# Two MLP layers whose tokens' operands leave out 1/rms, with Winograd products in the first block too

## The chip, the cores and the metric

One core of a Trainium2 chip runs the whole program in one launch. The metric is the device time of one execution in microseconds; the median of several executions counts.

## The reference

A trunk of two layers over 1024 tokens with 1024 features, all in float32: HGRN2 (a gated linear recurrence) and an MLP, then a shared compressed K/V, multi-head latent attention (MLA), a second MLP, and a last norm. What the change is about is the MLP, which occurs twice:

```python
def rmsnorm(x, gain):
    return x * lax.rsqrt(jnp.mean(x * x, axis=-1, keepdims=True) + EPS) * gain

def sq_relu_mlp(xn, w_up, w_down):                 # 1024 -> 4096 -> 1024
    return jnp.square(jax.nn.relu(xn @ w_up)) @ w_down

h = h + hgrn2_mixer(rmsnorm(h, ...), ...)
h = h + sq_relu_mlp(rmsnorm(h, mlp_norm[0]), mlp_w_up[0], mlp_w_down[0])
...
h = h + mla_mixer(rmsnorm(h, ...), ..., k_nope, k_rope, v, cos, sin)
h = h + sq_relu_mlp(rmsnorm(h, mlp_norm[1]), mlp_w_up[1], mlp_w_down[1])
return rmsnorm(h, final_norm)
```

1/rms is one positive number a token. It can therefore be taken out of the relu: relu(x r) = r relu(x), and out of the square as r squared.

## The kernel before

The tokens lie in two halves u = 0, 1 of 512; the stream `hT[u]` (tile `res` in the profile) holds the features on the partitions, in 8 tiles of 128x512. The stages follow one another: HGRN2 to about 672 us, the first MLP to 1345, K/V and attention to 2167, the second MLP and the last norm to the end. Within a stage a scheduler puts the instructions of each engine into one order ahead of time, by the order in which the code states them, by `tc.issue_after`, and by the rooms of the pools; at run time every engine works its queue in order.

**Products.** Every float32 operand is used as a high part (a cast to the matmul's type) and a low part (what the cast leaves out, by a subtraction); a product is three terms, high by high, high by low, low by high. `product` (L620) multiplies 512 features by 128 columns of weights and 512 tokens so: 12 matmuls of 128x512. `times` (L751) does a product of `down`: 24 matmuls into four banks of PSUM, then four additions to the stream on VectorE (L758). `parts` (L610 the cast on ScalarE, L534 the subtraction on GpSimd or VectorE) makes a weight's two parts, `halves` (L583, L534) the tokens'. In the profile `wh`, `wl` are weights' parts, `wu` and `dn` the raw rooms of w_up and w_down, `hh`, `hl` the parts of `down`'s inner operands, `fr` the room of the inner features, and `xn`, `T2h`, ..., `T4l` the tokens' parts; `ps`, `mm` and `nb` are PSUM banks.

**An MLP** takes the 4096 inner features in 8 blocks of 512. In each, `up` makes the inner features in two halves of 256, by Winograd's scheme in 7 products of half-size blocks (of tokens' features B11, B21, B22 and sums T1 to T4, of weights A11 to A22 and sums), then relu and square; `down` takes w_down's quarters and the inner features' quarters through 7 products x1 to x7, in the order x1, x5, x3, x6, x7, x4, x2, whose results add up in two sets of banks p and q. The very first up is `up_plain`: 16 products without Winograd's sums, the first token half before the second. Ahead of it `inverse(u)` takes the squares of the half's features (L560), adds them, multiplies with ones (L565), takes the logarithm and exponential and one Newton step, and `normed` (L577) multiplies the stream by gain and 1/rms. In layer 1 `finish.turn` transposes the stream in place, so that `down` adds with the tokens on the partitions: 64 transposes (L1170) and 16 copies out of PSUM (L1174 VectorE, L1176 ScalarE); they lie in `up_plain`.

```python
def down(A, s, last):                               # before, L763
    x1 = operands(A11, B11)
    ...
    q = times(s, x1, True, [(0, 0)])
    p = times(1 - s, x5, True, [(1, 1)])
    times(p, x3, False, [(1, 0)])
    times(q, x6, False, [(1, 0)])
    times(q, x7, False, [(1, 1)])
    times(q, x4, False, [(0, 1)])
    times(1 - s, x2, True, [(0, 0)])
```

Of the kernel before, what the change touches and what calls it, by code (L numbers as in the profile page):

```python
# [8 lines left out]
F32 = mybir.dt.float32  # L9
# [46 lines left out]
def build(nc, tc, a):  # L56
# [26 lines left out]
    ones = const.tile([P, P], F32R, name="ones")  # L83
    onef = const.tile([P, P], F32, name="onef")
    V.memset(onef, 1.0)
    V.tensor_copy(out=ones, in_=onef)
    eps = const.tile([P, 1], F32, name="eps")
    V.memset(eps, EPS)
    masks = const.tile([P, 640], U8, name="masks")
    m_diag = masks[:, 0:128]  # L90
    m_h1 = masks[:, 128:192]
    m_h2 = (masks[:, 192:256], masks[:, 256:320])
    m_lv = {h: masks[:, 320 + 64 * i:384 + 64 * i] for i, h in enumerate(LEVELS)}
    tri = const.tile([P, P], U8, name="tri")
    negt = const.tile([P, P], F32, name="negt")
    V.memset(negt, NEG)
# [80 lines left out]
    with common("hg"), tc.tile_pool(name="hg", bufs=1, reuse_waits="tile") as hp, \  # L177
            tc.tile_pool(name="hgp", bufs=1, space=PSUM, reuse_waits="tile") as pp:
        gn = vecs[:, R_GN:R_GN + 1]
        o_all = [None, None]  # L180

# [60 lines left out]
        lb, oml = const.tile([P, 8], F32, name="lb"), const.tile([P, 8], F32, name="oml")  # L242
# [208 lines left out]
        DMA.dma_start(out=mf[:, :640 + P], in_=a["masks"])  # L451
        G.tensor_copy(out=masks, in_=mf[:, :640])
        G.tensor_copy(out=tri, in_=mf[:, 640:640 + P])
# [53 lines left out]
    def mlp(layer, gain, finish):  # L507
# [5 lines left out]
        with ExitStack() as pools:  # L513
            mt, md, mf, mu, mw, mh, mp = (pools.enter_context(tc.tile_pool(name=f"mlp{n}{layer}", bufs=1,
                                                                           reuse_waits="tile")) for n in "tdfuwhp")
# [29 lines left out]
            X["T2"], X["B12"] = extra("T2"), extra("T4")  # L545
# [3 lines left out]
            for u, t in enumerate((fr, dn)):  # L549
# [4 lines left out]
            inv = s_y[:, 0], s_z[:, 0]  # L554

            def inverse(u, mark=None):
                acc, s, y, t = s_a[:, 0], s_a[:, 1], inv[u], s_y[:, 1]
# [6 lines left out]
                if mark is None:  # L564
                    T.matmul(ps, onef, acc, start=True, stop=True)  # L565
                else:
                    with tc.high_priority(offset=1000), tc.issue_after(mark):
                        T.matmul(ps, onef, acc, start=True, stop=True)
# [12 lines left out]
            def halves(eng, key, src):  # L581
                for k in (slice(0, 2), slice(2, 4)):
                    S.copy(out=X[key][0][:, k], in_=src[:, k])  # L583
                    sub(eng, X[key][1][:, k], src[:, k], X[key][0][:, k].bitcast(F32))

            def combine(eng, out, x, y):
                for k in (slice(0, 2), slice(2, 4)):
                    sub(eng, out[:, k], x[:, k], y[:, k])
# [12 lines left out]
            inverse(0, marks[-5 if finish is None else -14])  # L601
            normed(0, 0)
            halves(V, "B11", f[0, 0])
            normed(1, 0)
            halves(V, "B21", f[1, 0])

            def parts(eng, x, room=None):
                wh, wl = room or (small("wh"), small("wl"))
# [19 lines left out]
            def relu(o, src=None):  # L628
                S.activation(out=o, in_=o if src is None else src, func=AF.Relu)
                square(o)  # L630

            def up_plain(A, C):


                tiles = [(1, 0), (1, 1), (0, 0), (0, 1)]
                acc = {}
                room = extra("T3")
                w = {}
                for n, (e, i) in enumerate(tiles):
                    w[n, 0] = parts(G, A[e][i, 0], tuple(r[:, n, :] for r in room))  # L640
                    w[n, 1] = parts(G, A[e][i, 1])

                def step(n, u, k):
                    return product(acc[n, u], w[n, k], ("B11", "B21", "B12", "B22")[2 * u + k], k == 0, k == 1)

                def out(n, u):
                    e, i = tiles[n]
                    relu(C[e][i, u], acc[n, u])

                done = {}  # L650
                for n in range(4):
                    acc[n, 0], = banks_of(0, 1)
                    for k in range(2):
                        done[n] = step(n, 0, k)
                if finish is not None:
                    finish.turn(0, banks_of, done[1])
                inverse(1)
                normed(0, 1)
                halves(V, "B12", f[0, 1])
                normed(1, 1)  # L660
                halves(V, "B22", f[1, 1])
                if finish is not None:
                    finish.turn(1, banks_of, done[3])
                order = (2, 3, 0, 1)
                for n, b in zip(order, banks_of(1)):
# [594 lines left out]
```

## Time and profile before

| | |
|---|---|
| median of 3 executions | 2860.11 us (2858.74 to 2861.86) |
| the profiled execution | 2864.55 us, its span 2862.8 us |
| TensorE (PE) busy | 2684.2 us, 94% |
| VectorE (DVE) busy | 1826.6 us, 64% |
| GpSimd (POOL) busy | 1307.0 us, 46% |
| ScalarE (ACT) busy | 1200.8 us, 42% |
| mean granted clock of TensorE | 0.976 |

The span runs from the first to the last instruction that the profiler saw; the execution's time adds what lies around it. Busy times count what an engine works on, with matmuls that overlap counted once; an engine that stands is idle until its releaser, the instruction whose semaphore ended the wait.

### The profile page before, as it was taken

What the parts mean: (1) busy time and instruction counts of PE and PEld (TensorE: products, weight loads), DVE (VectorE), ACT (ScalarE), POOL (GpSimd) and SP (SyncE); (2) the same over time, 40 slices, a digit from 0 to 9 for tenths busy, and PEclk for the clock granted to TensorE, in tenths of its full rate; (3) what the DMA queues carried; (4) which work ended last, traced back from release to release, by engine and by line L of the source; (5) the groups of instructions that cost most, each with busy time, mean ns of one, the idle gap of its engine ahead of it and who ended that gap; (6) DMA issues with size and microseconds to landing.
All of it is one profiled execution on the core that took longest, in us unless ns stands there. A gap on an engine that the chain in (4) does not pass through costs nothing.

```text
span 2862.8 us, 35195 instructions
## 1 busy us (share of the span) xinstructions
PE 2684.2 (94%) x13189; PEld 2209.5 (77%) x13189; DVE 1826.6 (64%) x2952; ACT 1200.8 (42%) x2254; POOL 1307.0 (46%) x841
## 2 busy tenths in 40 slices
PE   7999999898899999998899999999997899999997
PEld 6778877687678777886688888888875787787775
DVE  5676677655755555558766766666667855555557
ACT  4222223223444444446354444444443444444445
POOL 4222223352677777775321322222211577776776
PEclk9999999899999999999899999999998999999999
DMA  4111112141211111110211111111110111111111
GB/s 135 37 38 30 30 45 60 52 127 36 64 55 52 52 52 52 60 55 25 68 28 38 32 43 47 30 47 28 49 34 19 56 56 49 54 54 59 56 44 67
DMA packets 184490, 144.00 MB, mean 50 GB/s; under 512 B 12482, under 2 KB 155903, under 8 KB 184319
## 3 DMA queue, kind: packets, MB, share of 16 engines
q1 hardware_dynamic: 184318, 141.75, 16.7%
q8 instruction: 104, 1.70, 0.3%
q14 instruction: 68, 0.55, 0.1%
HBM read 133.33 MB, written 4.19 MB: 48 GB/s over the span
## 4 chain that ended last, share of the span: by engine, by line
PE 70%; DVE 16%; issue 4%; ACT 4%; POOL 3%; DMA 2%; SPq 0%; DVEq 0%; POOLq 0%; ACTq 0%
PE mm L108 20%; PE ps L620 11%; PE mm L620 10%; PE ps L751 7%; PE s L1053 5%; PE mm L751 4%; PE nb L1086 3%; PE mm L1093 2%; POOL wl L534 2%; PE x L368 2%; DVE hl L534 2%; DVE fr L534 2%; PE nb L751 1%; DMA dn<-mlp_w_down 1%; DVE res L758 1%
## 5 line engine op out<-in xcount | busy, mean ns | idle before, releaser
L108 PE MATMUL mm<-xn,wh 128*128 128x512 f32 x1728 | 571.4, 405 | 8.2 <-DVE oh L906 3.8
L534 POOL TENSOR_TENSOR wl<-dn,wh 128x512 fp32r<-128x512 f32 x224 | 353.4, 1597 | 212.3 <-DVE hl L534 107.6
L108 PEld LDWEIGHTS mm<-xn,wh 128*128 128x128 f32 x1728 | 322.5, 191 | 71.6 <-issue 7.0
L108 PE MATMUL mm<-xn,wl 128*128 128x512 f32 x864 | 347.7, 402 | 0.0
L147 POOL TENSOR_TENSOR wl<-wst,wh 128x1024 fp32r<-128x1024 f32 (+1 forms) x93 | 220.6, 2375 | 244.8 <-ACT wh L144 242.0
L734 ACT CAST hh<-fr 128x1024 fp32r<-128x1024 f32 x110 | 115.8, 1053 | 257.3 <-PE ps L751 148.6
L534 POOL TENSOR_TENSOR wl<-wu,wh 128x512 fp32r<-128x512 f32 x144 | 199.3, 1392 | 42.7 <-PE ps L620 26.7
L534 POOL TENSOR_TENSOR wu<-wu,wu 128x512 f32<-128x512 f32 x112 | 157.1, 1403 | 123.8 <-DVE wl L534 83.1
L758 DVE TENSOR_TENSOR res<-res,ps 128x512 f32<-128x512 f32 x256 | 173.0, 686 | 59.3 <-PE ps L751 59.2
L1062 POOL TENSOR_SCALAR P<-P,rc 128x128 f32<-128x128 f32 (+1 forms) x64 | 52.1, 814 | 346.6 <-DVE rc L1060 316.3
L534 DVE TENSOR_TENSOR hl<-fr,hh 128x1024 fp32r<-128x1024 f32 x110 | 180.3, 1648 | 27.9 <-ACT hh L734 27.9
L534 POOL TENSOR_TENSOR dn<-dn 128x1024 f32<-128x1024 f32 x64 | 167.0, 2609 | 63.7 <-PE ps L751 39.8
L610 ACT CAST wh<-wu 128x512 fp32r<-128x512 f32 x200 | 122.0, 618 | 172.2 <-PE nb L751 52.7
L108 PEld LDWEIGHTS mm<-xn,wl 128*128 128x128 f32 x864 | 164.9, 191 | 32.0 <-issue 1.1
L1059 ACT ACTIVATE P<-s,mx 128x384 f32<-128x384 f32 (+7 forms) x128 | 95.2, 744 | 141.8 <-DVE mx L1057 121.3
L610 ACT CAST wh<-dn 128x512 fp32r<-128x512 f32 x224 | 130.1, 616 | 55.7 <-POOL dn L534 32.0
L534 DVE TENSOR_TENSOR fr<-fr 128x1024 f32<-128x1024 f32 x58 | 112.5, 1939 | 62.4 <-ACT fr L626 61.4
L1086 PE MATMUL nb<-h,xn 128*128 128x256 f32 (+1 forms) x640 | 138.1, 294 | 0.1
L100 ACT CAST h<-mm 128x512 fp32r<-128x512 f32 (+1 forms) x160 | 83.1, 546 | 105.7 <-PE mm L1093 105.7
L620 PE MATMUL ps<-xn,wh 128*128 128x512 f32 x512 | 126.8, 389 | 0.0
L146 POOL TENSOR_SCALAR wh<-wst 128x1024 fp32r<-128x1024 f32 (+2 forms) x57 | 63.1, 1111 | 131.3 <-PE mm L108 84.2
L620 PE MATMUL mm<-xn,wh 128*128 128x512 f32 x496 | 122.5, 389 | 0.0
(370 smaller groups left out, 6886.3 us busy)
## 6 DMA issues: line engine op xcount, KB each, us to landing
dn<-mlp_w_down SPq DMA_DIRECT2D x64, 512.0 KB, 3.8
wu<-mlp_w_up SPq DMA_DIRECT2D x122, 256.0 KB, 2.9
wst<-hgrn_w_o SPq DMA_DIRECT2D x16, 512.0 KB, 4.1
wst<-mla_w_o SPq DMA_DIRECT2D x16, 512.0 KB, 3.9
wst<-hgrn_w_q SPq DMA_DIRECT2D x10, 512.0 KB, 4.2
wst<-hgrn_w_i SPq DMA_DIRECT2D x10, 512.0 KB, 4.1
wst<-hgrn_w_g SPq DMA_DIRECT2D x10, 512.0 KB, 4.2
wst<-hgrn_w_f SPq DMA_DIRECT2D x9, 512.0 KB, 4.1
```

The costliest lines, as they stand in the source:

```text
L100: S.copy(out=out_h, in_=src)
L108: m = T.matmul(ps, l, r, start=i == 0, stop=i == n - 1)
L147: G.tensor_tensor(out=wl[:, cs], in0=st[:, cs], in1=wh[:, cs].bitcast(F32), op=ALU.subtract)
L534: eng.tensor_tensor(out=out, in0=x, in1=y, op=op)
L610: S.copy(out=wh, in_=x)
L620: m = T.matmul(bank, l[:, k, :], r[:, k, :], start=start and n == 0, stop=n == 11, skip_group_check=not start)
L734: cast = S.copy(out=hh, in_=Bq)
L751: T.matmul(banks[i], l, r, start=start and k == 0 and n == 0, stop=k == 1 and n == 2, skip_group_check=not start)
L758: V.tensor_tensor(out=o, in0=o, in1=banks[i], op=ALU.add)
L1053: T.matmul(ps[:, at + u * HALF:at + u * HALF + w_], l, r, start=e == 0, stop=e == len(terms) - 1)
L1059: S.activation(out=pt[:, :n], in_=sc, func=AF.Exp, bias=mx, accum_out=sm)
L1086: T.matmul(dst, l, r[:, cols_], start=j == 0 and e == 0, stop=j == 2 * g + 1 and e == 2)
```

## The change

1. *Operands without 1/rms.* `normed` goes. `gained` (ScalarE, times the gain) and `halves_of_stream` make the tokens' operands from the stream. Layer 0 still computes 1/rms as a row (`inverse`), but multiplies the inner features with it: relu becomes one VectorE instruction, max with 0 and times the row, where ScalarE did it. In layer 1 relu stays on ScalarE; `squares` gives the mean squares per token, with the tokens on the partitions, and `add` multiplies each sum by 1/ms when it adds it to the stream.
2. *`up_first` instead of `up_plain`:* both halves of 256 inner features together, by Winograd's 7 products each: 14 products instead of 16.
3. *`down`:* the products in the order x1, x5, x6, x3, x7, x2, x4, so that no product goes into the banks of its predecessor; the first set of banks alternates with the block. The last block keeps its order.
4. *`finish.turn`* stands after the T2 products and takes two `ps` and two `mm` banks; its copies alternate between ScalarE and VectorE.
5. *Rooms:* the tokens' halves change places in `dn` and `fr`; T3 and T4 have rooms of their own; the masks, a matrix of ones and small vectors live in the HGRN2 stage alone, and the attention stage loads its 128 columns of masks again (64 KB).

```diff
-            def normed(h, u):
+            def squares(u):
+                us = slice(4 * u, 4 * u + 4)
+                for c in range(4):
+                    for e in range(2):
+                        S.activation(out=s_a[:, 0], in_=hT[u][:, 4 * e + c, :], func=AF.Square,
+                                     accum_out=sq[:, 4 * u + c, e:e + 1])
...
+            def gained(h, u):
                 for k in range(4):
-                    V.scalar_tensor_tensor(out=f[h, u][:, k, :], in0=hT[u][:, 4 * h + k, :],
-                                           scalar=vecs[:, gain + 4 * h + k:gain + 4 * h + k + 1], in1=inv[u],
-                                           op0=ALU.mult, op1=ALU.mult)
+                    S.activation(out=f[h, u][:, k, :], in_=hT[u][:, 4 * h + k, :], func=AF.Copy,
+                                 scale=gains[4 * h + k])
...
+            def halves_of_stream(key, h, u):
+                for k in range(4):
+                    xh, xl = X[key][0][:, k, :], X[key][1][:, k, :]
+                    x, g = hT[u][:, 4 * h + k, :], gains[4 * h + k]
+                    S.activation(out=xh, in_=x, func=AF.Copy, scale=g)
+                    V.scalar_tensor_tensor(out=xl, in0=x, scalar=g, in1=xh.bitcast(F32), op0=ALU.mult,
+                                           op1=ALU.subtract)
...
-            def relu(o, src=None):
-                S.activation(out=o, in_=o if src is None else src, func=AF.Relu)
+            def relu(u, o, src=None):
+                src = o if src is None else src
+                if finish is None:
+                    V.scalar_tensor_tensor(out=o, in0=src, scalar=0.0, in1=row[:, u], op0=ALU.max, op1=ALU.mult)
+                else:
+                    S.activation(out=o, in_=src, func=AF.Relu)
                 square(o)
-            def up_plain(A, C):
...
+            def up_first(A, C):
...
+                first = each("B11", x, w, True)
...
+                each("B21", y, w, True)
+                halves("T1", f[0, 1])
+                halves_of_stream("B22", 1, 1)
+                if finish is None:
+                    inverse(1, first)
...
+                mark = each("T1", z, w, True)
...
+                w = [parts(V, A[e][0, 1]) for e in two]
+                z2 = [banks_of(0, 1)[0], nbank()]
+                each("B22", z2, w, True)
...
+                mark = each("T2", x, w, False)
...
+                if finish is not None:
+                    for u in range(2):
+                        finish.turn(u, banks_of, mark)
+                        squares(u)
+                each("T3", x, w, False)
...
+                    product(x[e], w[e], "T4", False, True)
+                    relu(0, C[e][1, 0], x[e])
...
+            def add(u, d, i, bank):
+                o = hT[u][:, 4 * d + i, :]
+                if finish is None:
+                    V.tensor_tensor(out=o, in0=o, in1=bank, op=ALU.add)
+                else:
+                    V.scalar_tensor_tensor(out=o, in0=bank, scalar=inv2[:, 4 * u + i:4 * u + i + 1], in1=o,
+                                           op0=ALU.mult, op1=ALU.add)
...
+                    x6 = operands(A21, B12)
+                    p = times(1 - s, x5, True, [(1, 1)])
...
                     x3 = operands(A11, B22)
...
-                    times(p, x3, False, [(1, 0)])
+                    times(q, x6, False, [(1, 0)])
...
-                    times(q, x6, False, [(1, 0)])
+                    times(p, x3, False, [(1, 0)])
...
+                    x2 = operands(A12, B21)
+                    times(q, x7, False, [(1, 1)])
                     x4 = operands(A22, B22)
-                    times(q, x7, False, [(1, 1)])
-                    x2 = operands(A12, B21)
+                    times(1 - s, x2, True, [(0, 0)])
                     times(q, x4, False, [(0, 1)])
-                    times(1 - s, x2, True, [(0, 0)])
...
-                banks = banks_of(1)
+                banks = banks_of(0, 2) + banks_of(1, 2)
...
-                    if c == 3 or u and c == 1:
+                    if c % 2:
```

How it moves instructions, at three places. First GpSimd (POOL) from the end of one `down` into the next `up`; `dn` is w_down's room, and a row `dn<-dn` a sum of two quarters. Before, from the subtractions for x7 on:

```order
L534 TENSOR_TENSOR wl_1368_7339<-dn_5636,wh_1367_7338 128x512
L534 TENSOR_TENSOR wl_1370_7343<-dn_5636,wh_1369_7342 128x512
L534 TENSOR_TENSOR wl_1374_7380<-dn_5636,wh_1373_7379 128x512
L534 TENSOR_TENSOR wl_1376_7384<-dn_5636,wh_1375_7383 128x512
L534 TENSOR_TENSOR dn_5636<-dn_5636 128x1024
L534 TENSOR_TENSOR wl_1380_7420<-dn_5636,wh_1379_7419 128x512
L534 TENSOR_TENSOR wl_1382_7424<-dn_5636,wh_1381_7423 128x512
L534 TENSOR_TENSOR wl_1388_7488<-wu_1329_7179,wh_1387_7487 128x512
L534 TENSOR_TENSOR wu_1331_7181<-wu_1331_7181,wu_1329_7179 128x512
```

Now:

```order
L531 TENSOR_TENSOR wl_1288_6776<-dn_5634,wh_1287_6775 128x512
L531 TENSOR_TENSOR wl_1290_6780<-dn_5634,wh_1289_6779 128x512
L531 TENSOR_TENSOR wl_1294_6817<-dn_5634,wh_1293_6816 128x512
L531 TENSOR_TENSOR wl_1296_6821<-dn_5634,wh_1295_6820 128x512
L531 TENSOR_TENSOR wl_1300_6857<-dn_5634,wh_1299_6856 128x512
L531 TENSOR_TENSOR wl_1302_6861<-dn_5634,wh_1301_6860 128x512
L531 TENSOR_TENSOR wl_1308_6925<-wu_1249_6616,wh_1307_6924 128x512
L531 TENSOR_TENSOR dn_5634<-dn_5634 128x1024
L531 TENSOR_TENSOR wu_1251_6618<-wu_1251_6618,wu_1249_6616 128x512
L531 TENSOR_TENSOR wu_1250_6617<-wu_1250_6617,wu_1251_6618 128x512
```

The sum of the next block's quarters (`dn<-dn`, the last one above) stood ahead of the last two weights' parts of the block; now it stands behind all of them and behind the next up's first, and ahead of that up's own sums of `wu`.

Second TensorE in layer 0's first up, where the ones matmul of the second half's 1/rms comes (`onef`, `one1` are the ones, `hh` the summed squares). Before:

```order
L620 MATMUL ps_1127_5795<-xn_1096_5628,wh_1122_5716 128x512 x4
L620 MATMUL ps_1127_5795<-xn_1098_5630,wh_1122_5716 128x512 x4
L620 MATMUL ps_1127_5795<-xn_1096_5628,wl_1123_5717 128x512 x4
L565 MATMUL nb_1128_5835<-hh_1104_5638,onef_73 128x512
L620 MATMUL mm_1129_5859<-T4h_1102_5634,T3h_1114_5694 128x512 x2
L620 MATMUL mm_1130_5860<-T4h_1102_5634,T3h_1114_5694 128x512
L620 MATMUL mm_1129_5859<-T4h_1102_5634,T3h_1114_5694 128x512 x2
```

Now:

```order
L646 MATMUL mm_1134_5823<-xn_1097_5625,wh_1131_5818 128x512 x4
L646 MATMUL mm_1134_5823<-xn_1099_5627,wh_1131_5818 128x512 x4
L646 MATMUL mm_1134_5823<-xn_1097_5625,wl_1132_5819 128x512 x4
L646 MATMUL ps_1139_5868<-xn_1097_5625,wh_1135_5860 128x512 x2
L569 MATMUL nb_1128_5804<-hh_1106_5636,one1_72 128x512
L646 MATMUL ps_1139_5868<-xn_1097_5625,wh_1135_5860 128x512 x2
L646 MATMUL ps_1139_5868<-xn_1099_5627,wh_1135_5860 128x512 x4
L646 MATMUL ps_1139_5868<-xn_1097_5625,wl_1136_5861 128x512 x4
```

It stood between the two token halves, ahead of every product of the second; now it stands after 2 matmuls of the seventh product (B22's first), with no product that needs its result behind it.

Third TensorE in layer 1's first up, where the stream is transposed (`res`, with `ident`). Before, the end of it:

```order
L1170 MATMUL mm_3736_18915<-ident_67,res_1047_5278 128x128 x4
L565 MATMUL nb_3734_18890<-hh_3702_18645,onef_73 128x512
L1170 MATMUL mm_3737_18916<-ident_67,res_1047_5278 128x128 x4
L1170 MATMUL nb_3738_18917<-ident_67,res_1047_5278 128x128 x4
L1170 MATMUL mm_3739_18938<-ident_67,res_1047_5278 128x128 x4
L1170 MATMUL mm_3740_18939<-ident_67,res_1047_5278 128x128 x4
L1170 MATMUL mm_3741_18940<-ident_67,res_1047_5278 128x128 x4
L1170 MATMUL nb_3742_18941<-ident_67,res_1047_5278 128x128 x4
L620 MATMUL mm_3743_18962<-T4h_3700_18641,T3h_3712_18701 128x512 x4
```

Now:

```order
L1218 MATMUL ps_3773_19005<-ident_67,res_1047_5274 128x128 x4
L1218 MATMUL mm_3774_19006<-ident_67,res_1047_5274 128x128 x4
L1218 MATMUL mm_3775_19007<-ident_67,res_1047_5274 128x128 x4
L1218 MATMUL ps_3776_19028<-ident_67,res_1047_5274 128x128 x4
L646 MATMUL ps_3736_18735<-T3h_3719_18670,wh_3760_18937 128x512
L1218 MATMUL ps_3777_19029<-ident_67,res_1047_5274 128x128 x4
L646 MATMUL ps_3736_18735<-T3h_3719_18670,wh_3760_18937 128x512
L1218 MATMUL mm_3778_19030<-ident_67,res_1047_5274 128x128 x4
L646 MATMUL ps_3736_18735<-T3l_3720_18671,wh_3760_18937 128x512 x2
L1218 MATMUL mm_3779_19031<-ident_67,res_1047_5274 128x128 x4
L646 MATMUL ps_3736_18735<-T3l_3720_18671,wh_3760_18937 128x512 x2
```

The transposes stood between the token halves with nothing else among them but the ones matmul; now they stand after the T2 products, and 8 of T3's matmuls lie among them.

## Rows read from the trace of the kernel before

**Rows 1.** The page, part 1: busy us (share) xinstructions.
```profile
PE 2684.2 (94%) x13189; PEld 2209.5 (77%) x13189; DVE 1826.6 (64%) x2952; ACT 1200.8 (42%) x2254; POOL 1307.0 (46%) x841
```

**Rows 2.** The page, part 4: the chain that ended last, share by engine.
```profile
PE 70%; DVE 16%; issue 4%; ACT 4%; POOL 3%; DMA 2%; SPq 0%; DVEq 0%; POOLq 0%; ACTq 0%
```

**Rows 3.** Stretches a:b (us): length, busy of each engine, PEclk, DMA share, GB/s.
```profile
727.00:750.40 23.40, 15.49 (x48) 11.37 (x47) 16.82 (x13) 11.38 (x19) 20.05 (x10) 0.78 0.17 52
760.00:1345.00 585.00, 564.93 (x2451) 460.78 (x2450) 341.27 (x379) 283.19 (x467) 417.07 (x264) 0.99 0.17 52
829.66:908.36 78.70, 76.89 (x337) 62.84 (x337) 43.92 (x50) 36.47 (x58) 56.84 (x37) 1.00 0.18 54
2290.00:2790.00 500.00, 487.68 (x2127) 398.50 (x2126) 271.42 (x306) 231.88 (x363) 357.77 (x229) 1.00 0.17 53
```

**Rows 4.** PE in order of time, layer 0's MLP begins: start, us, instructions, [wait].
```profile
673.15 1.20 PE L620 MATMUL ps<-xn,T3h 128*128 128x512 f32 x4 [1.19 <-ACT T3h L610]
...
695.05 1.02 PE L565 MATMUL nb<-hh,onef 128*128 128x512 f32 x2
702.36 1.22 PE L620 MATMUL mm<-T4h,T3h 128*128 128x512 f32 x2 [6.29 <-ACT T4h L583]
...
731.36 0.79 PE L751 MATMUL ps<-hh,wl 128*128 128x512 f32 x1 [3.60 <-POOL wl L534]
...
750.45 0.47 PE L751 MATMUL mm<-hh,wh 128*128 128x512 f32 x1 [2.02 <-DVE res L758]
```

**Rows 5.** The same, layer 1's MLP begins.
```profile
2170.68 2.50 PE L620 MATMUL ps<-xn,T3h 128*128 128x512 f32 x5 [3.68 <-ACT xn L583]
...
2197.72 1.47 PE L1170 MATMUL mm<-ident,res 128*128 128x128 f32 x12
...
2220.17 1.22 PE L620 MATMUL mm<-T4h,T3h 128*128 128x512 f32 x2
...
2250.14 0.50 PE L751 MATMUL ps<-wl,hh 128*128 128x512 f32 x1 [2.72 <-POOL wl L534]
...
2261.19 0.47 PE L751 MATMUL mm<-wh,hh 128*128 128x512 f32 x1 [3.05 <-DVE res L758]
```

**Rows 6.** What PE waited for, 727 to 1345 us, then 2244 to 2800 us.
```profile
PE mm L751 <- DVE res L758: 10.4, 8, 3.0
PE mm L751 <- POOL wl L534: 6.7, 7, 1.1
...
PE mm L751 <- POOL wl L534: 8.8, 7, 2.0
PE mm L751 <- DVE res L758: 7.6, 7, 3.0
```

**Rows 7.** POOL in order of time, from one down into the next up.
```profile
842.48 3.06 POOL L534 TENSOR_TENSOR wl<-dn,wh 128x512 fp32r<-128x512 f32 x2 [2.37 <-ACT wh L610]
849.50 2.40 POOL L534 TENSOR_TENSOR dn<-dn 128x1024 f32<-128x1024 f32 x1 [3.96 <-PE ps L751]
851.86 2.97 POOL L534 TENSOR_TENSOR wl<-dn,wh 128x512 fp32r<-128x512 f32 x2
854.79 1.29 POOL L534 TENSOR_TENSOR wl<-wu,wh 128x512 fp32r<-128x512 f32 x1
```

**Rows 8.** Line 577 (ns: min/median/max), then DVE and POOL after 2167 us.
```profile
L577 DVE SCALAR_TENSOR_TENSOR fr<-res,vecs,hl x16: 739/746/1761, 655.5 to 2179.2; 128x512 f32<-128x512 f32 x16
...
2167.99 6.59 DVE L577 SCALAR_TENSOR_TENSOR fr<-res,vecs,hl 128x512 f32<-128x512 f32 x4
...
2170.63 3.40 POOL L534 TENSOR_TENSOR T3l<-wu,T3h 128x512 fp32r<-128x512 f32 x2
```

**Rows 9.** Copies, squares (ns: min/median/max); loads (part 6: KB, us).
```profile
L1176 ACT COPY res<-mm x10: 581/589/605, 2199.3 to 2220.0; 128x512 f32<-128x512 f32 x10
...
L560 ACT ACTIVATE hh<-res x32: 622/632/635, 624.2 to 2187.6; 128x512 f32<-128x512 f32 x32
...
dn<-mlp_w_down SPq DMA_DIRECT2D x64, 512.0 KB, 3.8
```

More of the change, by code (lines that the diff above doesn't have):

```diff
@@ L82, in build @@
     make_identity(nc, ident)
[L83 to L86, printed above, removed]
+    one1 = const.tile([P, 1], F32, name="one1")
+    V.memset(one1, 1.0)
+    onef = one1.broadcast_to([P, P])
     eps = const.tile([P, 1], F32, name="eps")
     V.memset(eps, EPS)
[L89 to L96, printed above, removed]
     vecs = const.tile([P, NROWS], F32, name="vecs")
@@ L180, in build @@
         o_all = [None, None]
+        masks = hp.tile([P, 640], U8, name="masks")
+        ones = hp.tile([P, P], F32R, name="ones")
+        V.tensor_copy(out=ones, in_=onef)
+        m_diag = masks[:, 0:128]
+        m_h1 = masks[:, 128:192]
+        m_h2 = (masks[:, 192:256], masks[:, 256:320])
+        m_lv = {h: masks[:, 320 + 64 * i:384 + 64 * i] for i, h in enumerate(LEVELS)}
         def sb(tag, bufs, shape=(P, 512), dt=F32):
@@ L563, in inverse @@
                 ps = nbank()
-                if mark is None:
+                with tc.high_priority(offset=1000), tc.issue_after(mark):
                     T.matmul(ps, onef, acc, start=True, stop=True)
-                else:
-                    with tc.high_priority(offset=1000), tc.issue_after(mark):
-                        T.matmul(ps, onef, acc, start=True, stop=True)
                 S.activation(out=y, in_=ps, func=AF.Ln, scale=1.0 / D, bias=eps)
@@ L600, in mlp, with parts @@
             A0, A1 = load_up(0), load_up(1, [raw(), s_b[:, 0], s_b[:, 1], s_z[:, 1]])
[L601 to L608, printed above, removed]
+            gained(0, 0)
+            halves("B11", f[0, 0])
+            gained(1, 0)
+            halves("B21", f[1, 0])
+            gained(0, 1)
+            combine(f[0, 1], f[0, 1], f[0, 0])
+            gained(1, 1)
+            combine(f[1, 1], f[1, 1], f[0, 1])
+            combine(f[0, 0], f[1, 1], f[0, 0])
+            combine(f[1, 0], f[1, 0], f[1, 1])
+            if finish is None:
+                inverse(0, marks[-2])
+            def parts(eng, x):
+                wh, wl = small("wh"), small("wl")
                 wh, wl = (t.rearrange("p (k c) -> p k c", k=x.shape[1]) if len(x.shape) == 3 else t for t in (wh, wl))
@@ L755, in times @@
                         for u, d in outs:
-                            o = hT[u][:, 4 * d + i, :]
-                            V.tensor_tensor(out=o, in0=o, in1=banks[i], op=ALU.add)
+                            add(u, d, i, banks[i])
                         if ended is not None:
@@ L830, in mlp @@
                     A1 = load_up(2 * fb + 1)
[L831 removed]
+                    up(A1, outs(1), 1 - st)
                 if not last:
                     A0 = load_up(2 * fb + 2)
[L834 removed]
+                down(down_A, st, last)
     mlp(0, R_MLP0, None)
```

149 lines of the change are left out of this document (75 added, 74 removed).

## The prediction

> **What bounds the kernel.** I read the page's totals first, then the chain that ended last, the table by stretches, and then TensorE's own order of time at the two places where an MLP begins. TensorE is busy 2684.2 us, 94% of the span [rows 1], and carries 70% of the chain, VectorE 16%, GpSimd 3% [rows 2]. So time is gained here only by fewer matmuls, or where TensorE stands. In the middle of layer 0's MLP it works 564.93 of 585.00 us, in layer 1's 487.68 of 500.00 [rows 3]; the inner blocks have little to give, and VectorE with 43.92 busy of 78.70 us a block and GpSimd with 56.84 have room [rows 3]. The beginnings are worse. From the first product of up to the third product of the first down, 673.15 to 750.45, go 77.3 us [rows 4]; in layer 1 the same, with 64 transposes between, takes from 2167.0 (the first matmul at 2170.68 has waited 3.68) to 2261.19, 94.2 us [rows 5].
>
> A steady matmul costs 564.93 / 2451 = 0.2305 us [rows 3]. Before, either beginning has 192 matmuls of up (16 products of 12) and 48 of the first two down products: 240 x 0.2305 = 55.3 us. So 22.0 us are lost in layer 0 and 38.9 in layer 1, transposes among them. In layer 0 the rows name 6.29 (operands of the second half, which wait for 1/rms), 1.02 for the ones matmuls, 3.60 and 2.02 for the first down [rows 4]; the rest is shorter waits and slow matmuls: the granted clock in the first down's beginning was 0.78, while that of the blocks behind is 0.99 [rows 3]. In layer 1 they name 3.68 for the first operands, 22.4 from the first transpose to the next product, 2.72 and 3.05 [rows 5].
>
> **The change, part by part.** All parts are sums against the profiled execution, 2864.55 us, which is 4.44 above the median of 2860.11.
>
> *Layer 0's beginning.* The first up goes from 16 products to 14, 24 matmuls fewer: 216 x 0.2305 = 49.8 us. Its first operands need only a gain and a cast, so it starts where the wait of 1.19 began, near 672.0 instead of 673.15 [rows 4]. What I leave as lost: the two ones matmuls, still there, 1.0; a wait ahead of them and of B22, 4.0; the first down's cast, 0.8, and its operands, 2.0 in all, where 3.60 is one wait of several now; slow matmuls 3.0, somewhat under half of the 9.1 that before loses unnamed. The 2.02 for VectorE's additions goes, since the third down product no longer follows into the banks that its predecessor filled. Sum 10.8, so the third down product starts at 672.0 + 49.8 + 10.8 = 732.6 instead of 750.45: **-18**. The 4.0 is the uncertain one: the squares, their 7 additions, T1's and B22's low halves and the weights' sums are all queued on VectorE in the 72 x 0.2305 = 16.6 us of the products ahead of B22. With undisturbed durations the ones matmuls would wait about 1.4; but VectorE's multiplications by 1/rms took 6.59 us for 4 beside GpSimd's subtractions, against a median of 0.746 each [rows 8], and with such durations the wait is 8. I take the middle. Bounds: -25 (1.4 for that wait, 2.3 for the rest) to -10 (8, all of before's down waits kept).
>
> *Layer 1's beginning.* No ones matmul and no 1/rms on the way. The 3.68 at the start goes, since the casts need no normalisation: 49.8 us of matmuls from 2167.0. B22's weights are subtracted on VectorE, which in this stretch shares with GpSimd: 4 us. The transposes come after the T2 products. Half of their 16 copies stay on ScalarE at 0.589 [rows 9], and the first half's 8 squares stand between them on that engine; at 0.632 each [rows 9] that is 8 x 0.59 + 8 x 0.63 = 9.8, and 2 for the first and last transpose around them; 8 matmuls of T3 lie inside, 1.8: 10 net against 22.4. The first down's casts stand behind the second half's squares and the relus on ScalarE: 3.9 with its operands. Slow matmuls 3. Sum 49.8 + 4 + 10 + 3.9 + 3 = 70.7, so the third product starts near 2238 instead of 2261.19: **-23**. Bounds: -31 (no wait at B22, 8 for the transposes, 4 for the rest, a little clock) to -12 (8, 14, 5, 5).
>
> *The blocks between.* Before, the third product of each down (x3) goes into the banks that x5 has just left and waits for VectorE to add them up; the seventh (x2) waits for GpSimd. The rows give 10.4 in 8 waits and 6.7 in 7 in layer 0, 7.6 in 7 and 8.8 in 7 in layer 1 [rows 6]. Of the first, 2.02 is counted above [rows 4] and 3.0, the longest, is in the last down, whose order stays; of the third, 3.05 is counted above [rows 5]. That leaves 5.4 + 6.7 + 4.6 + 8.8 = 25.5 us. In the new order no product follows into its predecessor's banks, so the 10.0 of VectorE go. The 15.5 of GpSimd arise because the next block's first sum (849.50) stands ahead of x2's weights and has waited 3.96 [rows 7]. The view puts that down to TensorE; it is the reload of A22, whose last read ends at 842.48 + 3.06 = 845.5, and a load lands 3.8 later [rows 7, 9]. Now the last weights of the block are ahead of it. I take 10 of the 15.5, because x4's weights are now last and cut from the same queue: **-20**. Bounds: -25.5 to -8.
>
> *Hidden parts.* The 64 multiplications by 1/rms in layer 0 leave ScalarE for VectorE: 8 a block at the 0.746 of line 577's passes [rows 8], 6.0 on top of 43.92 of 78.70 [rows 3]. Cover: 29 us idle; if it went, up to 6 a block would come out. In layer 1 the additions become multiply-adds, one pass as before: nothing. The masks' second load, 64 KB on SP's queue, waits for the attention stage's first 1/rms, with the stage's weights queued behind it: 0, bounds -3 to +3, as for all else in the HGRN2 and attention stages. The smaller constants and swapped rooms let the first w_down load start earlier, which nothing waits for.
>
> Sum: -18 - 23 - 20 = -61, or 2803.5 for an execution like the profiled one and **2799** for the median.
>
> **A rule against it.** In rows 8 VectorE's pass over two operands, 6.59 for 4, lies beside GpSimd's subtractions (2170.63). The Trainium skill (GPSIMD Engine Reference, 1. Specifications) says the two engines share their SBUF interfaces and names VectorE instructions with two SBUF inputs as contending. By it every operation that this change puts onto VectorE while GpSimd works is stretched; the page would then have the sum near -30, the first rival's. The trace agrees in that one stretch; elsewhere the passes of this line have a median of 0.746 [rows 8].
>
> **Rivals.** *VectorE and GpSimd slow one another* wherever up_first and the new order put both to work. From rows: the stretched pass is 1.65 against 0.746 [rows 8]. Then both beginnings come out at their upper bounds (-10, -12) and the blocks keep all but 8 us: -30, **2830**. For: GpSimd has 56.84 of 78.70 [rows 3]. Against: layer 0's blocks already run both engines together without TensorE standing. Even stretched like that, the 8 new passes cost 13 a block on VectorE and stay hidden. Chance 0.18.
>
> *All waits go:* -25, -31, -25: **2779**. Chance 0.13.
>
> *GpSimd becomes the bound*, the slower case. A22 is now read by the last product, x4, so its room is reloaded later; the load lands after 3.8 us [rows 9], the next block's sum waits for it, and the next up's sums for T2 are queued behind that sum on GpSimd. With the passes of before that costs nothing: load, sum at 2.40 and three passes of 1.3 [rows 7] take 10.1; T2, the third product, reads its low half after 24 + 8 matmuls, 7.4 us into up; so x4's second low half has to end 2.7 us before up begins, and x4's own product reads it 10 matmuls, 2.3 us, before. But nothing is left over there, and a block's 56.84 busy [rows 3] and 3.96 of waiting for the reload [rows 7] fill a block of 78.70 once GpSimd's passes stretch by 78.70 / 60.8 = 1.29. At 1.35, from VectorE's added two-operand passes, a block takes 82.1: 14 blocks x 3.4 = 48, less 22 from the beginnings at their upper bounds: +26, **2886**. Against: an untouched GpSimd idles 22 us in a block, and layer 1 gets no added VectorE passes. Chance 0.05.
>
> *The shortened up gives nothing*: the products wait for operands one by one, and only the blocks gain: -20, **2840**. Against: the operands now hang on no long chain at all. Chance 0.05.
>
> **How the numbers follow.** The forecast, -61 with 15 either way, has 0.57; the other rivals as given, 0.02 for no difference. A measurement of this kernel tells about 0.2%, 5.7 us, from no change. Faster: 0.57 + 0.18 + 0.13 + 0.05 = 0.93; same 0.02; slower 0.05. The range goes from 2776, just past the rival without waits, to 2832, just past the contended one; outside lie the last two rivals and the tails.
>
> **What the profile after would show.** Right: the first up's 168 matmuls; the third down product near 732 and 2238; at the third product of a block no wait for VectorE's additions, at the seventh none or a small one for GpSimd; GpSimd's wait for the reload behind x4's weights. Wrong: rows of over 8 us at B22 or at the ones matmuls, VectorE passes of 1.6 us as a rule, T2 waiting for GpSimd in the blocks, or transposes that take over 16 us.

## The result: 50 us faster, from the beginnings somewhat more than from the blocks

The changed kernel takes 2810.86 us (2806.46 to 2812.76, 4 runs) against 2860.99 before: a ratio of 0.9824, 95% interval 0.9807 to 0.9841, or 50 us. The forecast was 2799 in a range from 2776 to 2832. The profiled execution's span is 2811.0 us, 51.8 below that of before. The page, parts 1 and 4:

```profile
PE 2656.4 (95%) x13137; PEld 2190.9 (78%) x13137; DVE 1916.4 (68%) x2990; ACT 1179.1 (42%) x2256; POOL 1387.6 (49%) x865
...
PE 67%; DVE 13%; POOL 6%; issue 6%; ACT 6%; DMA 2%; SPq 0%; DVEq 0%; POOLq 0%; ACTq 0%
```

TensorE's share barely moved; GpSimd has doubled its share of the chain, and VectorE has 90 us more to do [rows 1, 2]. Where the time went is read from the starts of the products. In the table a *beginning* runs from an MLP's first product of up to the third product of its first down, *blocks* from there to the first down product of the last block; all is worked out from the start times in TensorE's timeline.

| profiled execution | layer 0 beginning | layer 0 blocks | layer 1 beginning | layer 1 blocks |
|---|---|---|---|---|
| before | 77.3 | 540.1 | 90.5 (and 3.7 waited ahead) | 543.8 |
| changed | 63.2 | 535.8 | 77.2 | 524.5 |
| difference | -14.1 | -4.3 | -17.0 with the 3.7 | -19.3 |

These add up to -54.7; the other stages have the remaining +2.9. Between profiles whose HGRN2 instructions are nearly the same, the first product of the MLP began anywhere from 670.3 to 676.2 us, so that remainder is no effect that can be read here.

TensorE in order of time, layer 0's beginning, which answers to [rows 4]:

```profile
673.96 1.62 PE L646 MATMUL mm<-xn,wh 128*128 128x512 f32 x6
...
698.41 2.07 PE L569 MATMUL nb<-hh,one 128*128 128x512 f32 x2 [7.05 <-DVE hh L566]
...
713.26 1.19 PE L646 MATMUL ps<-T3h,wh 128*128 128x512 f32 x4 [1.24 <-ACT fr L705]
...
727.08 0.50 PE L796 MATMUL ps<-hh,wl 128*128 128x512 f32 x1 [0.51 <-POOL wl L531]
...
740.71 0.50 PE L796 MATMUL ps<-hh,wl 128*128 128x512 f32 x1 [2.89 <-POOL wl L531]
```

And layer 1's, which answers to [rows 5]:

```profile
2168.01 1.21 PE L646 MATMUL mm<-xn,wl 128*128 128x512 f32 x4 [1.38 <-POOL wl L531]
...
2171.95 0.49 PE L646 MATMUL ps<-xn,wh 128*128 128x512 f32 x1 [1.10 <-DVE xn L602]
2180.29 2.08 PE L646 MATMUL ps<-xn,wl 128*128 128x512 f32 x4 [7.85 <-DVE wl L531]
...
2190.92 1.03 PE L1218 MATMUL ps<-ident,res 128*128 128x128 f32 x8
...
2200.48 1.09 PE L646 MATMUL ps<-T3h,wl 128*128 128x512 f32 x4
...
2213.53 0.50 PE L796 MATMUL ps<-wh,hh 128*128 128x512 f32 x1 [3.80 <-ACT wh L636]
```

The waits of before for 1/rms, 6.29 and 3.68 [rows 4, 5], are gone, the transposes take 9.6 us instead of 22.4, and each layer has one new large wait among the B22 products: 7.05 us at the ones matmul in layer 0, 7.85 us at B22's low weights in layer 1, both for VectorE.

One block of layer 0 (885.8 to 963.8) and one of layer 1; the columns are those of [rows 3]:

```profile
885.80:963.80 78.00, 76.70 (x337) 62.84 (x336) 53.26 (x58) 31.96 (x51) 60.39 (x36) 1.00 0.18 55
2371.30:2447.60 76.30, 76.30 (x337) 62.94 (x336) 46.25 (x50) 35.93 (x57) 58.33 (x36) 1.00 0.18 56
```

Layer 1's blocks are full: 336 matmuls in 76.3 us, 0.227 each, no wait. Layer 0's keep one. What TensorE waited for from 745 to 1290 us, then from 2229 to 2755, against [rows 6]:

```profile
PE mm L796 <- POOL wl L531: 4.3, 4, 1.1
PE ps L796 <- POOL wl L531: 2.3, 3, 1.1
...
PE ps L796 <- DVE hl L531: 0.3, 1, 0.3
PE mm L796 <- POOL wl L531: 0.3, 1, 0.3
```

The waits for VectorE's additions are gone in both layers, those for GpSimd in layer 1; in layer 0 a wait of about 1.06 stands in four of six inner blocks, no longer at the seventh product but at the fourth, x3.

### The profile page after: what moved, and what is told of

It reads as the page before. It is cut to its first block, busy times and chain, and to the rows that moved or that the text cites. A ratio compares the mean times of both kernels' runs of the same rounds, so it can differ in the third digit from the quotient of the medians.

```text
span 2811.0 us, 35207 instructions
## 1 busy us (share of the span) xinstructions
PE 2656.4 (95%) x13137; PEld 2190.9 (78%) x13137; DVE 1916.4 (68%) x2990; ACT 1179.1 (42%) x2256; POOL 1387.6 (49%) x865
## 3 DMA queue, kind: packets, MB, share of 16 engines
q8 instruction: 103, 1.69, 0.3%
## 4 chain that ended last, share of the span: by engine, by line
PE 67%; DVE 13%; POOL 6%; issue 6%; ACT 6%; DMA 2%; SPq 0%; DVEq 0%; POOLq 0%; ACTq 0%
PE mm L99 21%; PE ps L796 8%; PE ps L646 7%; PE mm L646 7%; PE mm L796 6%; PE s L1101 5%; PE nb L1134 3%; POOL wl L531 3%; PE nb L796 2%; PE mm L1141 2%; PE x L366 2%; POOL wu L531 2%; DMA dn<-mlp_w_down 1%; ACT P L1107 1%; DVE fr L531 1%
## 5 line engine op out<-in xcount | busy, mean ns | idle before, releaser
L531 POOL TENSOR_TENSOR wl<-dn,wh 128x512 fp32r<-128x512 f32 x224 | 368.8, 1666 | 132.3 <-ACT wh L636 118.7
L531 POOL TENSOR_TENSOR wl<-wu,wh 128x512 fp32r<-128x512 f32 x154 | 221.2, 1448 | 59.7 <-ACT wh L636 53.9
L531 POOL TENSOR_TENSOR wu<-wu,wu 128x512 f32<-128x512 f32 x120 | 175.5, 1462 | 110.7 <-DVE wl L531 41.8
L636 ACT CAST wh<-wu 128x512 fp32r<-128x512 f32 x212 | 128.0, 618 | 240.0 <-POOL wu L531 121.8
L531 DVE TENSOR_TENSOR hl<-fr,hh 128x1024 fp32r<-128x1024 f32 x110 | 202.1, 1846 | 18.2 <-ACT hh L770 17.9
L531 POOL TENSOR_TENSOR dn<-dn 128x1024 f32<-128x1024 f32 x64 | 175.9, 2748 | 42.4 <-DMA dn<-mlp_w_down 38.7
L1059 POOL TENSOR_TENSOR P<-P,sin 128x512 f32<-128x512 f32 x16 | 21.2, 1325 | 203.6 <-DMA P<-P 203.6
```

The source lines that it names most:

```text
L531: eng.tensor_tensor(out=out, in0=x, in1=y, op=op)
L636: S.copy(out=wh, in_=x)
```

## The experiments

Three questions: what the order of down's products brings by itself, why B22 waits, and why layer 0's blocks keep a wait. Differences of medians are against the before of the same comparison, 2857.75 to 2860.09 us, or against the changed kernel's 2810.86.

**1. The order alone.** The kernel before with down's new order and alternating banks:

```diff
-                    times(p, x3, False, [(1, 0)])
+                    times(q, x6, False, [(1, 0)])
...
-                    times(q, x6, False, [(1, 0)])
+                    times(p, x3, False, [(1, 0)])
...
+                    times(q, x7, False, [(1, 1)])
...
-                    times(q, x7, False, [(1, 1)])
...
+                    times(1 - s, x2, True, [(0, 0)])
                     times(q, x4, False, [(0, 1)])
-                    times(1 - s, x2, True, [(0, 0)])
...
-                last = fb == NB - 1
+                last, st = fb == NB - 1, fb % 2
...
-                down(down_A, 0, last)
+                down(down_A, st, last)
```

The lines that make the products' operands move with them.

> The kernel before with nothing but the new order of down's products and the banks that alternate with the block. Theory: the order alone takes away the waits for VectorE's additions, and with relu still on ScalarE in layer 0 it does so in both layers: layer 1's blocks 19 us shorter as in the changed kernel, layer 0's 10 to 18, and the third product of either first down 2 to 3 earlier. Total 2826 to 2834, that is 27 to 35 below before. Rival: the blocks' gain needs the other parts (w_down's room free earlier, rooms of T3 and T4): only 5 to 10 below before, 2851 to 2856.

Measured 2826.59, ratio 0.9891 [0.9870, 0.9912], 32 us below before. Every inner block of both layers takes 76.2 to 76.4 us; layer 0's blocks 529.1, layer 1's 528.2, which is 11.0 and 15.6 shorter (10 to 18 and 19 were expected). The beginnings are 71.1 and 86.5, 6.2 and 4.0 shorter, more than the 2 to 3 expected. The theory holds: the order needs none of the other parts, and it is the larger part of the gain.

**2. The change without the order** (the same edit the other way round, in the changed kernel).

> The changed kernel with the old order of down's products. Theory: what the order brought in the blocks, 23 us, comes back, and the beginnings keep their gain: 2832 to 2838. Rival: the blocks' gain is from elsewhere, then it stays: 2811 to 2816.

Measured 2848.53, ratio 0.9960 [0.9942, 0.9977]: beyond both expectations. Layer 1's blocks come back to 541.9 as foreseen, but layer 0's go to 553.9, 13.8 us *above* before. The beginnings are 67.3 and 79.9, 4.1 and 2.7 longer than in the changed kernel. TensorE's waits in layer 0's blocks, 745 to 1300 us:

```profile
PE mm L796 <- POOL wl L531: 9.1, 8, 2.0
PE mm L796 <- ACT hh L770: 4.6, 4, 1.1
PE mm L796 <- DVE res L780: 3.8, 2, 1.9
```

So some other part of the change costs layer 0's blocks 14 us, which the new order had hidden for the most part. Layer 1 has no such cost; what only layer 0 has is relu on VectorE. That makes relu the suspect; no run took it out under the old order.

**3. Relu back on ScalarE in layer 0** (without 1/rms there, so its output is another):

```diff
-                if finish is None:
-                    V.scalar_tensor_tensor(out=o, in0=src, scalar=0.0, in1=row[:, u], op0=ALU.max, op1=ALU.mult)
-                else:
-                    S.activation(out=o, in_=src, func=AF.Relu)
+                S.activation(out=o, in_=src, func=AF.Relu)
```

> The changed kernel with layer 0's relu on ScalarE as in layer 1; the multiplication by 1/rms is left out in layer 0, so the output is another. Theory: in layer 0's blocks x3 waits 1.06 us for GpSimd because VectorE's two-operand relus stretch GpSimd's passes and hold up ScalarE's queue; without them the wait goes and a block takes 76.3 to 76.8 as in layer 1, where 78.1 stand now: 5 to 9 us less, 2802 to 2806. Rival: GpSimd is late in layer 0 by its own queue: within 2 us of the changed kernel.

Measured 2799.89, 11 below the changed kernel, 2 past the expectation; layer 0's inner blocks 76.2 to 76.3, all of them, 529.4 in layer 0's blocks together (535.8). The 6.4 us in the blocks are the relus' cost under the new order. Of the rest of the 11, 3.7 in the profiles lie ahead of the first MLP, where the two kernels do not differ. How the cost comes about, the changed kernel's trace shows where a block's up passes into down. ScalarE first, then GpSimd:

```profile
885.75 0.63 ACT L652 ACTIVATE fr<-fr 128x512 f32<-128x512 f32 x1 [1.95 <-DVE fr L657]
886.28 0.60 ACT L636 CAST wh<-dn 128x512 fp32r<-128x512 f32 x1
...
886.96 1.82 POOL L531 TENSOR_TENSOR wl<-dn,wh 128x512 fp32r<-128x512 f32 x1 [1.80 <-ACT wh L636]
888.87 5.75 POOL L531 TENSOR_TENSOR dn<-dn 128x1024 f32<-128x1024 f32 x2
894.58 3.54 POOL L531 TENSOR_TENSOR wl<-dn,wh 128x512 fp32r<-128x512 f32 x2
898.20 3.28 POOL L531 TENSOR_TENSOR dn<-dn 128x1024 f32<-128x1024 f32 x1
901.44 7.05 POOL L531 TENSOR_TENSOR wl<-dn,wh 128x512 fp32r<-128x512 f32 x4
```

ScalarE's square waits for VectorE's relu, x5's cast stands behind the square, GpSimd waits 1.80 for the cast and has no gap after that until x3's low halves at 901.44. A queue in order passes VectorE's lateness on to an engine that does not need relu at all. It is not the whole of it. Counted from the down's first matmul and compared with the block of layer 1 above, the pass behind the cast starts 0.9 us later here (1.2 for 0.3), and x3's low halves 2.0 us later (15.7 for 13.7). The other 1.1 are two of the GpSimd passes between that last longer beside VectorE, 1.82 for 1.60 and 3.28 for 2.42. Experiment 3 takes both causes away together; only this comparison of traces divides them.

**4. 24 matmuls more in either beginning**, ahead of B22:

```diff
+                each("T1", z, w, True)
                 mark = each("T1", z, w, True)
```

> The changed kernel with the two T1 products of each first up computed twice, 24 matmuls more in each layer, in front of the B22 products. Theory: TensorE waits there 7.05 and 7.85 us for VectorE, so 24 x 0.227 = 5.4 us of matmuls in each layer disappear in the wait: 0 to 3 us in all, 2811 to 2814; and the 24 matmuls that the change leaves out brought nothing by themselves. Rival: matmuls bound the beginning: 10.9 us more, 2822.

Measured 2809.57, 1.3 below the changed kernel, which is no difference; the beginnings are 65.1 and 78.0, 2.7 longer in all where 10.9 us of matmuls were added. TensorE's wait at B22 in layer 1 fell from 7.85 to 0.62, with new ones of 1.78 and 1.34 at the transposes; in layer 0 the ones matmul began 24.0 us after the first product, as before (24.5). But only 3 of the 24 matmuls lie ahead of it there, and its wait is still 6.25; the other 21, 4.8 us of matmuls, lengthen the stretch from it to the first down by 2.4. So here the matmuls that the change saves are worth about a quarter of their time.

**5. B22's weights first** in VectorE's queue, and layer 0's second squares behind them:

```diff
-                if finish is None:
-                    inverse(1, first)
...
-                halves("T2", f[1, 1])
-                halves("T3", f[0, 0])
...
                 w = [parts(V, A[e][0, 1]) for e in two]
+                halves("T2", f[1, 1])
                 z2 = [banks_of(0, 1)[0], nbank()]
-                each("B22", z2, w, True)
+                last = each("B22", z2, w, True)
+                if finish is None:
+                    inverse(1, last)
+                halves("T3", f[0, 0])
```

> The changed kernel with VectorE's queue in the first up put in the order of need: B22's weights ahead of T2's and T3's low halves, and in layer 0 the second half's squares and ones matmul behind them. Theory: the waits of 7.05 and 7.85 us at B22 are VectorE's queue, not the operands: both shrink to 0 to 2, 10 to 13 us less in all, 2798 to 2801. Rival: VectorE and GpSimd together are full in this stretch, so T2 or T3 waits instead: 0 to 4 less.

Measured 2807.18, 4 less: the rival. The waits at B22 go, and others come (TensorE's rows, layer 0 and layer 1):

```profile
708.94 2.07 PE L646 MATMUL ps<-T3h,wh 128*128 128x512 f32 x4 [9.47 <-ACT fr L705]
...
2183.01 1.09 PE L1218 MATMUL ps<-ident,res 128*128 128x128 f32 x4 [4.34 <-DVE fr L707]
```

Layer 0's beginning is 65.9, 2.7 longer, layer 1's 72.4, 4.8 shorter. (The expectation of 9 below has 68.3 and 74.6 for them. Those run to a later matmul of the third product, behind its first waits; by the table's rule it is 65.9 and 72.4.)

**6. No second 1/rms in layer 0** (`inverse(1, first)` taken out, the first half's row used for both).

> The changed kernel without the second half's 1/rms in layer 0 (squares, 7 additions, ones matmul, Newton step left out; the first half's factor is used for both, so the output is another). Theory: layer 0's beginning loses the wait of 7.05 at the ones matmul and the matmul itself, but B22's weights then still stand behind T2's and T3's halves, as in layer 1: 4 to 7 us less, 2804 to 2807, and layer 1 the same as before. Rival: GpSimd's weights hold B22 as much: 0 to 2 less.

Measured 2806.01, in the middle of the expectation; layer 0's beginning 58.7, 4.5 shorter, with 4.21 left at B22.

**7. Squares of layer 1 later**, on top of 5 (`squares(1)` behind the first up):

> The kernel with B22's weights first, and in layer 1 the second half's squares behind the first up instead of among its relus. Theory: the first down's wait of 3.80 for ScalarE's casts falls to about 1, as in layer 0: 2 to 3 us below the kernel with B22's weights first alone, 2795 to 2799. Rival: ScalarE is late there by relu and square themselves: no difference between the two.

Measured 2808.47, no difference from 5, which is the rival; the wait for ScalarE's casts is still 3.80.

**8. A21 minus A11 on VectorE** in layer 0's blocks, on top of 7:

```diff
-                    sub(G, A21, A21, A11)
+                    sub(V if finish is None else G, A21, A21, A11)
```

> The kernel with both of these edits, and in layer 0's blocks one sum of w_down's quarters (A21 minus A11) on VectorE instead of GpSimd. Theory: GpSimd's queue is 2 us late at x3 in layer 0, and the sum takes 2.9 of it: x3's wait of 1.06 goes in the blocks where it stood, 4 to 7 us less than without this edit, 2790 to 2794. Rival: VectorE waits with the sum for GpSimd's last part of A21 and holds up x6's inner operand: x6 waits instead, 0 to 10 us more.

Measured 2803.25, 5.2 below 7; every inner block of layer 0 takes 76.2 to 76.7 and x3's wait is gone. That agrees with the reading of 3.

**9 and 10. Relus held behind the copies of T2's banks** (`tc.issue_after` on the copy), with 5 and 8; in the second of them layer 0 keeps its order of halves and squares.

> The kernel with B22's weights first, with A21 minus A11 on VectorE in layer 0, and with the first up's relus of its first tiles held behind ScalarE's copies of the T2 banks. Theory: with B22 first TensorE waited 9.5 us at T3 (layer 0) and 4.3 at the transposes (layer 1) for those copies, which stood behind squares that wait for VectorE; held behind, both fall to 0 to 3 us. Layer 0's beginning 60 to 63 us (68.3 with B22 first alone, 63.2 in the changed kernel), layer 1's 70 to 72 (74.6, 77.2); with the blocks of the sum on VectorE 2791 to 2797. Rival: the passes themselves fill VectorE, GpSimd and ScalarE, and the wait moves to T4 or the first down: the beginnings stay within 2 us of those with B22 first alone, 2800 to 2804.

> The same, but layer 0's first up keeps the changed kernel's order of T2's and T3's halves and of the second half's squares; B22's weights come first in layer 1 alone. Theory: layer 0's beginning as in the changed kernel, 62 to 64, since 1/rms then is early and the relus behind it are not late; layer 1's 70 to 72 as in the run beside it: 2792 to 2799. Rival: as there, layer 1's beginning 74 to 75: 2799 to 2803.

Measured 2805.21 and 2800.48. The wait at T3 in layer 0 fell from 9.47 to 2.15, but 5.42 came up at the ones matmul, and in layer 1 the transposes still wait 4.91 and 3.76, the first down 5.09 and 5.07. Beginnings 65.0 and 76.2, 64.4 and 75.7, against 65.9 and 72.4 in 5: layer 0's hardly moved, layer 1's became 3 to 4 longer. The first run lies above both its ranges, the second in its rival's. The theory that holding the relus back would end these waits fell here; most of what one order won at one place was lost at another.

**11. GpSimd out of the beginnings.** What all these queues share is VectorE without a gap from 2152.7 to 2186.4 us, and passes that take about twice their usual time or more. So the opposite of relief: all of up_first's weights' passes, 20 in each layer, go to VectorE.

```diff
-                w = [parts(G, A[e][0, 0]) for e in two]
+                w = [parts(V, A[e][0, 0]) for e in two]
...
-                    sub(G, A[e][1, 0], A[e][1, 0], A[e][1, 1], ALU.add)
+                    sub(V, A[e][1, 0], A[e][1, 0], A[e][1, 1], ALU.add)
```

and so on for every `G` in it.

> The changed kernel with all sums and low halves of the weights of either first up on VectorE instead of GpSimd: 20 passes of 128x512 more on VectorE in each layer, 0.69 us each undisturbed, 13.8 in all. Theory: VectorE and GpSimd stretch each other's two-operand passes (0.69 to 1.75, 1.22 to 2.3 in the changed kernel), 12 us of VectorE's 34 in layer 1's beginning; alone it does its own passes at 0.69 and 1.22 and most of GpSimd's in the time saved: the wait at B22 stays within 4 us of 7, the beginnings within 4 us of 63.2 and 77.2, and passes of 1.7 us are gone: 2807 to 2819. Rival: VectorE's passes are slow for another reason or its queue is simply full: each beginning 10 to 14 us longer, 2831 to 2839.

Measured 2797.16 (2796.32 to 2799.99), ratio 0.9791 [0.9774, 0.9807]: 14 below the changed kernel, better than the theory asked for. The beginnings are 57.6 and 70.7, 5.6 and 6.5 shorter, though VectorE has 20 passes more. VectorE's groups in layer 1's beginning, of the changed kernel (2152.7 to 2186.4 us):

```profile
L602 DVE SCALAR_TENSOR_TENSOR xn<-res,vecs,xn 128x512 fp32r<-128x512 f32 x4 | 6.8, 1766 | 0.0
L531 DVE TENSOR_TENSOR dn<-dn,fr 128x1024 f32<-128x1024 f32 x2 | 4.6, 2318 | 0.0
...
L531 DVE TENSOR_TENSOR T3l<-dn,T3h 128x1024 fp32r<-128x1024 f32 x2 | 4.5, 2278 | 0.0
```

and the same with GpSimd out of it (2144.5 to 2180.4):

```profile
L602 DVE SCALAR_TENSOR_TENSOR xn<-res,vecs,xn 128x512 fp32r<-128x512 f32 x4 | 2.7, 743 | 0.0
...
L531 DVE TENSOR_TENSOR dn<-dn,fr 128x1024 f32<-128x1024 f32 x2 | 2.4, 1214 | 0.0
...
L531 DVE TENSOR_TENSOR T3l<-dn,T3h 128x1024 fp32r<-128x1024 f32 x2 | 2.3, 1214 | 0.0
```

The same passes over the same operands take 743 instead of 1766 ns, 1214 instead of 2318. That GpSimd's work stretches these passes is shown by taking it away. B22's waits fall to 3.51 and 2.16 with it, now for ScalarE's casts. How much of the 12 us comes from the stretch alone is not separated, since the 20 passes that moved are shorter on VectorE too, 0.69 for 1.30 us, and TensorE gets their weights sooner.

**12. All that helped**: 11, with B22's weights first and the sum of 8.

> The kernel with the first ups' weights on VectorE, and two edits more: B22's sums and weights ahead of T2's and T3's halves in VectorE's queue, and in layer 0's blocks A21 minus A11 on VectorE. Theory: without GpSimd beside it VectorE has room, so the order of need now pays where it did not before: the 3.51 and 2.16 us that B22 waits for its weights go, layer 0's beginning 54 to 56 us (57.6 with the weights on VectorE alone), layer 1's 67 to 69 (70.7); and x3's wait in layer 0's blocks goes, 530 to 531 for 534.6: 2786 to 2791. Rival: as in the runs with B22 first alone, the wait moves on to T3 or the first down, and only the blocks gain: 2792 to 2795.

Measured 2793.15 (2788.13 to 2796.31, 5 runs), ratio 0.9776 [0.9762, 0.9790], the lowest median of all, though the interval overlaps that of 11. Layer 0's blocks are 532.1 (534.6 in 11); the beginnings, 57.3 and 71.3, did not shorten, so the rival was right about them: layer 1's first down now waits 5.74 for ScalarE's casts, where 3.81 stood.

## Why the prediction was right, and where it was not

**Right in sum and in kind.** The range and the sign hold, no block waits for VectorE's additions, layer 1's transposes and first operands no longer wait, and T2 never waits for GpSimd's reload in the blocks: the slower rival did not come up. The terms were off both ways, though: the beginnings gave 10 us less than forecast and the blocks 4 more. And one sign of being wrong that the prediction names, VectorE passes of 1.6 us as a rule, did come up in layer 1's beginning.

**Layer 0's beginning, -18:** it was -14.1, or -15.3 from where TensorE became free. Of the 10.8 us left as lost, the wait at the ones matmul was put at 4.0, as the middle between 1.4 and 8, which is 4.7; it measured 7.05. The term was mis-sized, and it alone makes the difference, 63.2 us for 60.6 from the first product on. The stretch that I had read from one row as an exception [rows 8] is common where the two engines meet on SBUF operands, and the trace of before had it in other lines too: of VectorE's `hl<-fr,hh`, 1.22 us alone, the 34 that lie almost wholly beside GpSimd's passes take 1.69 on the mean. The third down product began at 737.19 instead of 732.6, of which 2.0 is a later start of the MLP, at 673.96 instead of 672.0.

**Layer 1's beginning, -23:** it was -17.0. B22's 4 was 7.85, with 1.38 and 1.10 ahead of it; the first down's 3.9 was 3.80 and 0.61. The transposes were better than put: 7.8 net of the T3 matmuls for 10. What is left over, slow matmuls, is about 5 for 3.

**The 24 matmuls** were subtracted at full price, 49.8 for 55.3 us, with VectorE's wait added as a separate term. Experiment 4 shows in layer 1 that these are not two terms: the wait there is a date set by VectorE, so matmuls ahead of it come out of the wait. In layer 0 most of the added matmuls stand behind the wait and cost half their time; which later waits took up the other half is not separated. So the smaller number of products did little. The new order of down brought 4.1 and 2.7 of the beginnings' gain (experiment 2); that the rest comes from the end of the chain through 1/rms and of the transposes' waits is read from the rows, not tested by itself.

**The blocks, -20:** it was -23.6, but split as 19.3 in layer 1 and 4.3 in layer 0, where the waits of before were 4.6 + 8.8 = 13.4 and 5.4 + 6.7 = 12.1. In layer 1 they all went, and the short gaps behind them too. That the sum came out near is in part luck: I had left 5.5 us for GpSimd at x4, which did not come, and relu cost 6.4, which I had put at nothing. The step that failed is under *hidden parts*: 64 relus on VectorE at nothing, since 29 us of VectorE's block are idle. VectorE did stay below its limit, 53.26 of 78.00. But its room was the wrong question: what counts is when the relu ends, since ScalarE's queue hands that lateness to GpSimd, and when VectorE's passes and GpSimd's hold one another up. It costs 6.4 us under the new order (experiment 3); under the old one layer 0's blocks were 13.8 above before (experiment 2), and relu is the likely cause there, inferred and not tested. And I had expected what remains at x4, the last to be cut; it remains at x3.

**The first rival**, contention, had 0.18 and 2830. Its mechanism is the true one in the beginnings, which gave back about 10 of the 41 expected there, not the half that it was priced at; in the blocks it did not decide in layer 1, and in layer 0 it is part of the 6.4 us, beside the way through ScalarE's queue. Beside it, the Trainium skill (GPSIMD Engine Reference, 1. Specifications) names VectorE instructions with two SBUF inputs as contending with GpSimd; experiment 11 agrees with it, 1766 against 743 ns.

## What to carry to other kernels

A pass moved to an idle engine is not free because the engine has room: follow which queue its end date enters, and what unrelated work stands behind it there. Where VectorE and GpSimd both work on SBUF operands in a short, dense stretch, price each pass at its own time and what is left of the other engine's pass, and try giving all of it to VectorE: here 20 passes more on VectorE in either beginning made it 6 us shorter. And an accumulation that goes back into the banks that were just filled waits for whoever empties them; alternating the order of independent products cost nothing and brought 32 us by itself.

## What the runs showed of the hardware

The stretch goes both ways. VectorE's groups of passes over two SBUF operands take up to 2.4 times as long beside GpSimd, and GpSimd's own 128x512 sums 2.24 us instead of 1.30 (rows of the changed kernel):

```profile
2177.45 2.24 POOL L531 TENSOR_TENSOR wu<-wu,wu 128x512 f32<-128x512 f32 x1
...
2188.64 1.30 POOL L531 TENSOR_TENSOR wu<-wu,wu 128x512 f32<-128x512 f32 x1 [1.01 <-DMA wu<-mlp_w_up]
```

It is a wait for turns and not a lower rate. In the block above, GpSimd's sum runs from 892.23 to 894.62; VectorE's pass begins 0.25 us into it and ends 1.09 us after it:

```profile
892.23 2.39 POOL L531 TENSOR_TENSOR dn<-dn 128x1024 f32<-128x1024 f32 x1
892.48 3.23 DVE L531 TENSOR_TENSOR hl<-fr,hh 128x1024 fp32r<-128x1024 f32 x1 [0.21 <-ACT hh L770]
```

From the first product of either MLP to its last down, 166 VectorE passes over two SBUF operands began while a GpSimd pass ran and took longer than alone. Every one ended 1.08 to 1.09 us (109 passes of 128x1024) or 0.55 us (57 of 128x512) after that GpSimd pass, whatever was left of it. GpSimd's passes that began in such a VectorE pass ended at least 1.1 us after it. So what a pass pays is the rest of the other engine's pass, and two dense queues take turns.

Passes with one operand in PSUM do not show it. In the block above, while GpSimd worked from 888.87 to 894.6, VectorE's four additions of a bank to the stream took 2.47 us together, no more than four of the 0.686 that they take on the mean in the kernel before; and none of layer 0's 224 such additions took more than 0.69, though 94 of them lie wholly inside a GpSimd pass:

```profile
889.80 2.47 DVE L780 TENSOR_TENSOR res<-res,ps 128x512 f32<-128x512 f32 x4
```
